# Eight instead of sixteen of a convolution's taps on TensorE, its shifted rows made through device memory, its places one or two slots later

## The chip, the cores and the metric

The kernel runs on one core of a Trainium2 chip. Its time is the device time of one execution in microseconds (us). TensorE (PE) multiplies matrices into PSUM, VectorE (DVE) and ScalarE (ACT) work element by element, GpSimdE (POOL) fills borders and issues some transfers, SyncE (SP) issues most transfers. Every engine works off its own list of instructions, and semaphores hold an instruction back until what it needs is done.

## The reference, cut to what matters

A backbone of two layers works on 640 tokens (128 of a prompt, 512 of a sample) of 1024 channels. Each layer is a feed-forward block, a mixer and a feed-forward block. The mixer of the second, odd layer is this; its depthwise convolution over 31 neighbouring tokens is what the change is about:

```python
def gmlp_conv_mixer(h, w_in, v_ln_g, v_ln_b, sp_w, sp_b, dw_w, dw_b, cn_g, cn_b, w_out):
    u, v, ga, gg = jnp.split(h @ w_in, [D_C, 2 * D_C, 2 * D_C + D_D], axis=-1)
    u = jax.nn.gelu(u)
    v = layer_norm(jax.nn.gelu(v), v_ln_g, v_ln_b)
    vc = v.reshape(b, L // MLP_CHUNK, MLP_CHUNK, N_HEADS_C, HEAD_DIM_C)
    sv = jnp.einsum('hts,bcshd->bcthd', sp_w, vc) + sp_b.T[None, None, :, :, None]
    y_c = u * sv.reshape(b, L, D_C)
    glu = ga * jax.nn.sigmoid(gg)
    y_d = jax.nn.silu(layer_norm(depthwise_conv_centred(glu, dw_w, dw_b), cn_g, cn_b))
    return jnp.concatenate([y_c, y_d], axis=-1) @ w_out
```

## The kernel before, in words

Channels lie on the 128 partitions, tokens along the free axis, so 1024 channels are eight blocks `j`. Tokens are worked in two halves of 320, A and B. All large products are made of three products of rounded halves: a weight tile `wr` is loaded by SP, ScalarE rounds it to `wh` (L217), VectorE takes the rest `wl = wr - wh` (L218), and TensorE multiplies `wh` and `wl` with both halves of the activations (`mm3`, L383 to L385). A unit is one weight tile; two units ahead of the current one are loaded and split.

In `odd`, TensorE's list runs thus. For each block `j` it makes `ga` and `gg` of half A, then of half B; `glu_post` gates them into `pads[j]`, 685 columns with zero borders. Then comes the value product in two rounds of four steps (L1340 to L1342, five PSUM banks at once), then eight `u` units, each followed from the third on by one gate product `sv` (L1360), then the output product, ahead of whose first unit the layer norm's sums over all eight convolution outputs stand (L1396).

Between these stand numbered slots; `bg(slot)` puts convolution `j` at the slot that `CONV_AT` gives: slots 0 to 5 stand behind half A of blocks 2 to 7, slots 6 to 13 behind the eight steps of the value product, slots 14 to 21 among the `u` units. `conv(j)` has three parts. TensorE makes the first `PE_TAPS` taps: four taps at a time, as four row groups of 32 partitions of a tile `R` hold the same 32 channels shifted by 0 to 3 columns, multiplied with a small diagonal matrix `dg` of the tap weights (L1276; 32 instructions a convolution). ScalarE adds the bias and writes `ac` (L1279). VectorE adds the other taps, one scalar_tensor_tensor of 655 columns each (L1283), the last of them in two pieces into `co[j]` (L1288). `rep_next` (L1254) prepares the next convolution's `R` by 16 small copies from SBUF to SBUF (L1261) and its `dg` by one product on VectorE (L1264). One convolution is prepared ahead (`REPS`).

What sets the order: TensorE's list is that of the code. The lists of the other engines are set at build time by a scheduler that goes by priorities; the taps on VectorE have a lowered one (`CONV_LATE`), so the scheduler puts other work first where it reckons it to be ready. At run time each list is worked off as it stands. Tiles called `slab`, `pad`, `cacc`, `diag` share one pool of `OB` buffers (tag `"s"`); PSUM has eight banks.

Of the kernel before, what the change touches and what calls it, by code (L numbers as in the profile page):

```python
# [10 lines left out]
F32 = mybir.dt.float32  # L11
# [5 lines left out]
P = 128  # L17
# [14 lines left out]
NSTD = 3  # L32
TAP_EARLY = 400
NORM_EARLY = 200
PE_TAPS = 16
RW = 655 + PE_TAPS - 4
REPS = 1
OB = 21
XW_EARLY = 600
CONV_LATE = 3000  # L40
CONV_AT = (1, 2, 3, 4, 5, 7, 9, 11)
SV_LAG = 2
LN_STEPS = ((0, 'sum', 0), (0, 'sum', 1), (0, 'mean', 0), (0, 'mean', 1), (3, 'sq', 0), (5, 'sq', 1), (7, 'var', 1), (11, 'var', 0))
Y_AT = (1, 3)
# [28 lines left out]
def build(tc, ap):  # L73
    nc = tc.nc
    V, S, TE, G = nc.vector, nc.scalar, nc.tensor, nc.gpsimd
    ctx = ExitStack()
    with ctx:
# [4 lines left out]
        spool = ctx.enter_context(tc.tile_pool(name="slabs", bufs=8))  # L82
        tpool = ctx.enter_context(tc.tile_pool(name="temps", bufs=10))
        pspool = ctx.enter_context(tc.tile_pool(name="psum", bufs=8, space=PSUM))
        state = {"pool": None, "ctx": None}

        uid = [0]

        def nm(p):
            uid[0] += 1  # L90
            return f"{p}_{uid[0]}"

        def slab(dt=F32, cols=T):
            return state["pool"].tile([P, cols], dt, tag="s", name=nm("slab"))
# [32 lines left out]
        def open_phase(bufs):  # L127
            state["ctx"] = ExitStack()
            state["pool"] = state["ctx"].enter_context(tc.tile_pool(name=nm("phase"), bufs=bufs, reuse_waits="tile"))
# [11 lines left out]
        def psum(cols=512):  # L141
            return pspool.tile([P, cols], F32, tag="ps", name=nm("ps"))
# [13 lines left out]
        def cvc(name, i):  # L156
            o = CV[name] + i
            return cv[:, o:o + 1]
# [310 lines left out]
        def boundary(first_keys, L, isc, ish, prev, kind):  # L469
            need_mod(L, isc)  # L470
            need_mod(L, ish)
            hn = []

            def nxt(H, rs, cs):
                if cs[0] == 0 and H == A:
                    prefetch(index[first_keys[-1]])
                    hn.append(kind())
                for c in cs:
                    if H == A and c < 2:
                        with tc.high_priority(offset=NORM_EARLY):  # L480
                            apply_mod(H, c, rs, L, isc, ish, hn[0])
                    else:
                        apply_mod(H, c, rs, L, isc, ish, hn[0])
            prev(nxt)

            def mid():
                nxt(B, finish(B), range(KC))
            pa = run_units(A, first_keys, hn[0], kouter=True, mid={1: mid})
            close_phase()
            return hn[0], pa  # L490
# [736 lines left out]
        def odd(prev):  # L1227
            first = [("oga", 0), ("ogg", 0), ("oga", 1), ("ogg", 1)]
            hn, pa = boundary(first, 1, 4, 3, prev, Rows)
            open_phase(OB)  # L1230
            ph = state["pool"]
# [12 lines left out]
            pads = {}  # L1244
# [9 lines left out]
            def rep_next():  # L1254
                if not ready or len(reps) == REPS:
                    return
                j = ready.pop(0)
                R = [ph.tile([P, RW], F32, tag="s", name=nm("rep")) for _ in range(4)]
                for r in range(4):
                    for q in range(4):  # L1260
                        nc.sync.dma_start(out=R[q][32 * r:32 * r + 32, :], in_=pads[j][32 * q:32 * q + 32, r:r + RW])  # L1261
                ng = PE_TAPS // 4
                dg = ph.tile([P, ng * 4, 32], F32, tag="s", name=nm("diag"))
                V.tensor_mul(dg, id4[:, None, :].to_broadcast([P, ng * 4, 32]),  # L1264
                             cw[:, j, 0:ng].rearrange("p m q -> p (m q)")[:, :, None].to_broadcast([P, ng * 4, 32]))
                reps[j] = (R, dg)

            def conv(j):
                pad = pads.pop(j)
                R, dg = reps.pop(j)  # L1270
                ac = ph.tile([P, 655], F32, tag="s", name=nm("cacc"))
                for q0, q1 in ((0, 328), (328, 655)):
                    ps = psum()
                    for m in range(PE_TAPS // 4):
                        for q in range(4):
                            TE.matmul(ps[32 * q:32 * q + 32, :q1 - q0], lhsT=dg[:, 4 * m + q, :],  # L1276
                                      rhs=R[q][:, 4 * m + q0:4 * m + q1],
                                      start=(m == 0), stop=(m == PE_TAPS // 4 - 1))
                    S.activation(out=ac[:, q0:q1], in_=ps[:, :q1 - q0], func=AF.Identity, bias=cvc("dw_b", j))  # L1279
                rep_next()  # L1280
                with tc.high_priority(offset=-CONV_LATE):
                    for i in range(PE_TAPS, CONV_D - 1):
                        V.scalar_tensor_tensor(out=ac, in0=pad[:, i:i + 655], scalar=cvc("dw_w", i * 8 + j), in1=ac,  # L1283
                                               op0=ALU.mult, op1=ALU.add)
                    co[j] = slab(F32)
                    i = CONV_D - 1
                    for a, b, d in ((0, 128, 0), (128, 640, 15)):
                        V.scalar_tensor_tensor(out=co[j][:, a:b], in0=pad[:, a + d + i:b + d + i],  # L1288
                                               scalar=cvc("dw_w", i * 8 + j), in1=ac[:, a + d:b + d],
                                               op0=ALU.mult, op1=ALU.add)  # L1290

            def bg(slot):
                for j, at in enumerate(CONV_AT):
                    if at == slot:
                        conv(j)

            def glu_post(H, j, pga, pgg):
                if H == A:
                    t = ph.tile([P, 685], F32, tag="s", name=nm("pad"))
                    for a, b in ((0, 15), (143, 158), (670, 685)):  # L1300
                        G.memset(t[:, a:b], 0.0)
                    pads[j] = t
                sg = tmp()
                S.activation(out=sg, in_=pgg[:, :TH], func=AF.Sigmoid)
                o = SL[H].start
                for (a, b, cond) in SEGS[H]:
                    d = a + 15 if cond == 1 else a + 30
                    V.tensor_mul(pads[j][:, d:d + b - a], sg[:, a - o:b - o], pga[:, a - o:b - o])
                if H == B:
                    ready.append(j)  # L1310
                    rep_next()
# [257 lines left out]
```

## Time and profile before

| | |
|---|---|
| median of 3 runs | 2646.93 us (2642.45 to 2650.54) |
| profiled execution | 2652.95 us, its span 2651.2 us |
| mean granted clock of TensorE | 0.988 |
| ScalarE, GpSimdE busy | 47%, 6% of the span |
| transfers | 378.09 MB, mean 143 GB/s |

The span runs from the first to the last instruction of the profiled execution. A busy time is the time in which an engine had an instruction at work; a wait is the idle time just before an instruction, put down to the one that released it last. The granted clock is the share of TensorE's full clock that the chip allowed.

### The profile page before, as it was taken

The numbers are of one execution on the slowest core, as the hardware profiler recorded it, in microseconds if no ns is written. First come the engines' busy times: TensorE is split into PE (matmuls) and PEld (weight loads), VectorE is DVE, ScalarE is ACT, GpSimd is POOL, SyncE is SP. The second block draws the span as 40 slices with busy tenths as digits, with TensorE's granted clock in tenths as the row PEclk, the third lists the DMA queues.
The fourth block names the chain that finished last, engine by engine and source line by source line (L and its number), as shares of the span: only waits on it lengthen the run. The fifth ranks groups of instructions, "written<-read, shape, count | busy, mean of one in ns | idle before, by whom it ended". The sixth has DMA issues, their size and how long they took to land. (4 is left out here: it accounts for less than half of the span.)

```text
span 2651.2 us, 43728 instructions
## 1 busy us (share of the span) xinstructions
PE 2526.2 (95%) x17229; PEld 2435.4 (92%) x17229; DVE 1936.4 (73%) x3265; ACT 1236.3 (47%) x2310; POOL 154.3 (6%) x255
## 2 busy tenths in 40 slices
PE   7899999899999999999999999999999999999997
PEld 5899999889989999999989999989879998999997
DVE  6878878689996967777597777856885749554465
ACT  4434535458863544445354444533223535444452
POOL 0010110000000010101001011000000000101100
PEclk9999999999999999999999999999999999999999
DMA  7477886222112376877248687724442124656651
GB/s 286 126 215 194 221 222 168 79 70 64 47 54 88 108 200 180 214 195 187 82 125 208 185 227 202 190 80 135 135 110 64 56 72 125 162 144 146 155 123 58
DMA packets 140078, 378.09 MB, mean 143 GB/s; under 512 B 17504, under 2 KB 24160, under 8 KB 139360
## 3 DMA queue, kind: packets, MB, share of 16 engines
q1 hardware_dynamic: 111568, 296.33, 35.4%
q0 software_dynamic: 24768, 71.31, 15.2%
q10 hardware_dynamic: 3536, 7.66, 0.9%
q8 instruction: 135, 2.21, 0.3%
q14 instruction: 71, 0.58, 0.1%
HBM read 329.17 MB, written 3.67 MB: 126 GB/s over the span
## 5 line engine op out<-in xcount | busy, mean ns | idle before, releaser
L218 DVE TENSOR_TENSOR wl<-wr,wh 128x1024 fp32r<-128x1024 f32 (+3 forms) x393 | 390.8, 997 | 301.9 <-ACT wh L217 110.7
L217 ACT CAST wh<-wr 128x1024 fp32r<-128x1024 f32 (+3 forms) x393 | 340.1, 868 | 369.1 <-DMA wr<-in_wd 113.8
L385 PE MATMUL ps<-h,wl 128*128 128x320 f32 x1408 | 438.5, 311 | 9.8 <-DVE wl L218 9.8
L383 PE MATMUL ps<-h,wh 128*128 128x320 f32 x1408 | 438.6, 312 | 8.0 <-ACT h L367 7.9
L384 PE MATMUL ps<-h,wh 128*128 128x320 f32 x1408 | 437.8, 311 | 2.9 <-DVE h L368 2.9
L752 PE MATMUL ps<-th,wh 128*128 128x320 f32 x1216 | 384.0, 316 | 36.4 <-ACT tmp L734 24.5
L752 PE MATMUL ps<-quad,wh 128*128 128x320 f32 x1824 | 406.3, 311 | 1.6 <-ACT tmp L734 1.5
L752 PE MATMUL ps<-th,wl 128*128 128x320 f32 x1216 | 381.9, 314 | 3.7 <-DVE wl L218 3.7
L752 PE MATMUL ps<-tl,wh 128*128 128x320 f32 x1216 | 381.1, 313 | 0.0
L314 DVE CUSTOM_DVE_ANT_0 junk<-wm,crow,cv 128x1024 bf16<-128x1024 f32 x256 | 327.7, 1280 | 3.3 <-DMA wm<-in_wm 0.7
L383 PE MATMUL ps<-pair,wh 128*128 128x320 f32 (+1 forms) x976 | 307.6, 315 | 4.6 <-ACT pair L376 1.5
L752 PEld LDWEIGHTS ps<-quad,wh 128*128 128x128 f32 x1824 | 307.5, 189 | 2.3 <-ACT tmp L734 2.3
L384 PE MATMUL ps<-pair,wh 128*128 128x320 f32 (+1 forms) x976 | 302.7, 310 | 1.6 <-DVE pair L378 1.4
L385 PE MATMUL ps<-pair,wl 128*128 128x320 f32 (+1 forms) x976 | 302.4, 310 | 0.0
L752 PE MATMUL ps<-quad,wl 128*128 128x320 f32 x912 | 283.2, 311 | 4.7 <-DVE wl L218 4.7
L385 PEld LDWEIGHTS ps<-h,wl 128*128 128x128 f32 x1408 | 265.9, 189 | 14.0 <-DVE wl L218 14.0
L383 PEld LDWEIGHTS ps<-h,wh 128*128 128x128 f32 x1408 | 266.1, 189 | 10.2 <-ACT h L367 9.9
L752 PEld LDWEIGHTS ps<-th,wh 128*128 128x128 f32 x1216 | 232.9, 191 | 44.0 <-ACT tmp L734 30.8
L384 PEld LDWEIGHTS ps<-h,wh 128*128 128x128 f32 x1408 | 266.0, 189 | 5.0 <-DVE h L368 4.6
L218 DVE TENSOR_TENSOR wl<-ws,wh 128x1024 fp32r<-128x1024 f32 x152 | 185.6, 1221 | 90.7 <-ACT wh L217 38.5
L752 PEld LDWEIGHTS ps<-th,wl 128*128 128x128 f32 x1216 | 233.0, 192 | 5.5 <-DVE wl L218 5.5
L752 PEld LDWEIGHTS ps<-tl,wh 128*128 128x128 f32 x1216 | 232.9, 192 | 0.0
(261 smaller groups left out, 4380.4 us busy)
## 6 DMA issues: line engine op xcount, KB each, us to landing
wm<-in_wm SPq DMA_DIRECT2D x128, 512.0 KB, 4.4
wr<-in_wgu SPq DMA_DIRECT2D x76, 512.0 KB, 4.9
ws<-in_wgu SPq DMA_DIRECT2D x152, 256.0 KB, 4.2
ws<-in_wgu POOLq DMA_DIRECT2D x76, 512.0 KB, 6.0
x<-y POOLq DMA_DIRECT2D x96, 320.0 KB, 6.1
wr<-in_wd SPq DMA_DIRECT2D x64, 384.0 KB, 3.5
wr<-in_wd SPq DMA_DIRECT2D x64, 320.0 KB, 3.9
wr<-in_wgu SPq DMA_DIRECT2D x76, 256.0 KB, 3.7
```

What stands on the lines that cost most here:

```text
L217: S.copy(hi, src)
L218: state["paced"] = V.tensor_sub(lo, src, hi).ins
L314: V.tensor_tensor_reduce(out=junk[0], in0=w, in1=crow[cond], scale=1.0, scalar=cvc("b_mod", L * 72 + idx * KC + c), op0=ALU.mult, op1=ALU.add,
L383: TE.matmul(ps, lhsT=wh, rhs=xh, start=start, stop=False)
L384: TE.matmul(ps, lhsT=wh, rhs=xl, start=False, stop=False)
L385: TE.matmul(ps, lhsT=wl, rhs=xh, start=False, stop=stop)
L752: TE.matmul(ps[:, :TH], lhsT=l[k], rhs=r[:, k, :], start=(first and k == 0 and n == 0), stop=(k == 3 and n == 2), skip_group_check=True)
```

## The change

`PE_TAPS` goes from 16 to 8: TensorE's part of a convolution is 16 instructions instead of 32, and VectorE adds taps 8 to 30 instead of 16 to 30, that is 22 full-length instructions and the last tap in two pieces instead of 14 and the last. `R` is one tile with a buffer of its own; `rep_next` writes `pads[j]` to a `row` in device memory and reads it back by four transfers, one for each shift, that fill all four column groups. The pool of slabs has 17 instead of 21 buffers. The convolutions stand at slots 2, 3, 4, 5, 7, 9, 11, 13: the first to fourth one slot later, the last four two slots later.

```diff
--- before.py
+++ after.py
@@ -32,13 +32,13 @@
 NSTD = 3
 TAP_EARLY = 400
 NORM_EARLY = 200
-PE_TAPS = 16
+PE_TAPS = 8
 RW = 655 + PE_TAPS - 4
 REPS = 1
-OB = 21
+OB = 17
 XW_EARLY = 600
 CONV_LATE = 3000
-CONV_AT = (1, 2, 3, 4, 5, 7, 9, 11)
+CONV_AT = (2, 3, 4, 5, 7, 9, 11, 13)
 SV_LAG = 2
 LN_STEPS = ((0, 'sum', 0), (0, 'sum', 1), (0, 'mean', 0), (0, 'mean', 1), (3, 'sq', 0), (5, 'sq', 1), (7, 'var', 1), (11, 'var', 0))
 Y_AT = (1, 3)
@@ -82,6 +82,7 @@
         spool = ctx.enter_context(tc.tile_pool(name="slabs", bufs=8))
         tpool = ctx.enter_context(tc.tile_pool(name="temps", bufs=10))
         pspool = ctx.enter_context(tc.tile_pool(name="psum", bufs=8, space=PSUM))
+        dpool = ctx.enter_context(tc.tile_pool(name="rows", bufs=1, space=bass.MemoryType.DRAM))
         state = {"pool": None, "ctx": None}
 
         uid = [0]
@@ -1255,10 +1256,12 @@
                 if not ready or len(reps) == REPS:
                     return
                 j = ready.pop(0)
-                R = [ph.tile([P, RW], F32, tag="s", name=nm("rep")) for _ in range(4)]
+                R = ph.tile([P, 4, RW], F32, tag="rep", name=nm("rep"), bufs=REPS)
+                row = dpool.tile([P, 685], F32, tag="pad", name=nm("row"), bufs=2)
+                nc.sync.dma_start(out=row, in_=pads[j])
                 for r in range(4):
-                    for q in range(4):
-                        nc.sync.dma_start(out=R[q][32 * r:32 * r + 32, :], in_=pads[j][32 * q:32 * q + 32, r:r + RW])
+                    nc.sync.dma_start(out=R[32 * r:32 * r + 32, :, :],
+                                      in_=row[:, r:r + RW].rearrange("(q p) w -> p q w", p=32))
                 ng = PE_TAPS // 4
                 dg = ph.tile([P, ng * 4, 32], F32, tag="s", name=nm("diag"))
                 V.tensor_mul(dg, id4[:, None, :].to_broadcast([P, ng * 4, 32]),
@@ -1274,7 +1277,7 @@
                     for m in range(PE_TAPS // 4):
                         for q in range(4):
                             TE.matmul(ps[32 * q:32 * q + 32, :q1 - q0], lhsT=dg[:, 4 * m + q, :],
-                                      rhs=R[q][:, 4 * m + q0:4 * m + q1],
+                                      rhs=R[:, q, 4 * m + q0:4 * m + q1],
                                       start=(m == 0), stop=(m == PE_TAPS // 4 - 1))
                     S.activation(out=ac[:, q0:q1], in_=ps[:, :q1 - q0], func=AF.Identity, bias=cvc("dw_b", j))
                 rep_next()
```

The change also moves VectorE's list. In the rows below, `cacc` are taps, the last `slab` rows of a `cacc` its last tap, `wl` weight splits, `pad` gatings; the numbers are those of buffers. VectorE, before, at the second convolution (of `pad_18839`):

```order
L1283 SCALAR_TENSOR_TENSOR cacc_19367<-pad_18839,cv,cacc_19367 128x655 x2
L1264 TENSOR_TENSOR diag_19424<-id_18829,cw 128x512
L1283 SCALAR_TENSOR_TENSOR cacc_19367<-pad_18839,cv,cacc_19367 128x655
L218 TENSOR_TENSOR wl_19499<-wr_19496,wh_19498 128x1024
L1283 SCALAR_TENSOR_TENSOR cacc_19367<-pad_18839,cv,cacc_19367 128x655 x3
L218 TENSOR_TENSOR wl_19506<-wr_19503,wh_19505 128x1024
L1308 TENSOR_TENSOR pad_19359<-tmp_19493,ps_19443 128x320
L1283 SCALAR_TENSOR_TENSOR cacc_19367<-pad_18839,cv,cacc_19367 128x655 x8
L1288 SCALAR_TENSOR_TENSOR slab_19440<-pad_18839,cv,cacc_19367 128x128
```

After, from the second convolution's first taps (of `pad_18841`) on to the `diag` of the fourth:

```order
L1286 SCALAR_TENSOR_TENSOR cacc_19458<-pad_18841,cv,cacc_19458 128x655 x2
L219 TENSOR_TENSOR wl_19569<-wr_19566,wh_19568 128x1024
L1286 SCALAR_TENSOR_TENSOR cacc_19458<-pad_18841,cv,cacc_19458 128x655 x3
L1311 TENSOR_TENSOR pad_19450<-tmp_19563,ps_19513 128x320
L219 TENSOR_TENSOR wl_19576<-wr_19573,wh_19575 128x1024
L1286 SCALAR_TENSOR_TENSOR cacc_19458<-pad_18841,cv,cacc_19458 128x655 x17
L1291 SCALAR_TENSOR_TENSOR slab_19510<-pad_18841,cv,cacc_19458 128x128
L1311 TENSOR_TENSOR pad_19628<-tmp_19632,ps_19572 128x128
L1311 TENSOR_TENSOR pad_19628<-tmp_19632,ps_19572 128x192
L1267 TENSOR_TENSOR diag_19664<-id_18831,cw 128x256
```

Before, the `diag` for the third convolution stood two taps into the second and 14 taps ran in pieces of 2, 1, 3 and 8. Now 22 taps run in pieces of 2, 3 and 17, and the next `diag`, that of the fourth convolution, stands behind all of them.

VectorE, before, from the seventh convolution (`cacc_20330`), with the `diag` of the eighth in the second row:

```order
L1283 SCALAR_TENSOR_TENSOR cacc_20330<-pad_19757,cv,cacc_20330 128x655 x2
L1264 TENSOR_TENSOR diag_20387<-id_18829,cw 128x512
L1283 SCALAR_TENSOR_TENSOR cacc_20330<-pad_19757,cv,cacc_20330 128x655 x5
L218 TENSOR_TENSOR wl_20550<-wr_20547,wh_20549 128x1024
L1283 SCALAR_TENSOR_TENSOR cacc_20330<-pad_19757,cv,cacc_20330 128x655 x6
L218 TENSOR_TENSOR wl_20586<-wr_20583,wh_20585 128x1024
L1283 SCALAR_TENSOR_TENSOR cacc_20330<-pad_19757,cv,cacc_20330 128x655
L1288 SCALAR_TENSOR_TENSOR slab_20403<-pad_19757,cv,cacc_20330 128x128
L1288 SCALAR_TENSOR_TENSOR slab_20403<-pad_19757,cv,cacc_20330 128x512
```

After, from the sixth convolution (`cacc_20138`) to the `diag` of the eighth:

```order
L219 TENSOR_TENSOR wl_20374<-wr_20371,wh_20373 128x1024
L1286 SCALAR_TENSOR_TENSOR cacc_20138<-pad_19450,cv,cacc_20138 128x655 x16
L219 TENSOR_TENSOR wl_20478<-wr_20475,wh_20477 128x1024
L1286 SCALAR_TENSOR_TENSOR cacc_20138<-pad_19450,cv,cacc_20138 128x655 x4
L1349 BN_STATS vst<-vbig 128x6
L1286 SCALAR_TENSOR_TENSOR cacc_20138<-pad_19450,cv,cacc_20138 128x655
L1349 BN_STATS vst<-vbig 128x6 x4
L1351 BN_AGGR vmv<-vst 128x2 x5
L219 TENSOR_TENSOR wl_20537<-wr_20534,wh_20536 128x1024
L1291 SCALAR_TENSOR_TENSOR slab_20190<-pad_19450,cv,cacc_20138 128x128
L1291 SCALAR_TENSOR_TENSOR slab_20190<-pad_19450,cv,cacc_20138 128x512
L1267 TENSOR_TENSOR diag_20308<-id_18831,cw 128x256
```

The `diag` of the eighth convolution stood two taps into the seventh; now it stands ahead of the seventh's taps but behind all of the sixth's, with splits and norm steps among them.

VectorE, before, from the last taps of the eighth convolution to the first gate product:

```order
L1283 SCALAR_TENSOR_TENSOR cacc_20493<-pad_19956,cv,cacc_20493 128x655 x2
L1350 RECIPROCAL vrs<-vrs 128x5
L1288 SCALAR_TENSOR_TENSOR slab_20544<-pad_19956,cv,cacc_20493 128x128
L1352 TENSOR_SCALAR vbig<-vbig,vmv,vrs 128x1024 x5
L218 TENSOR_TENSOR wl_20762<-wr_20759,wh_20761 128x1024
L1288 SCALAR_TENSOR_TENSOR slab_20544<-pad_19956,cv,cacc_20493 128x512
L218 TENSOR_TENSOR wl_20834<-wr_20831,wh_20833 128x1024
L218 TENSOR_TENSOR wl_20906<-wr_20903,wh_20905 128x1024
L1365 SCALAR_TENSOR_TENSOR slab_20825<-ps_20818,cv,spb 128x384
L1365 SCALAR_TENSOR_TENSOR tmp_20828<-ps_20819,cv,spb 128x256
L1367 TENSOR_TENSOR slab_20672<-slab_20672,slab_20825 128x384
```

After, from the first tap of the eighth convolution to the first gate product (L1368 and L1370) and the next split:

```order
L1286 SCALAR_TENSOR_TENSOR cacc_20407<-pad_19806,cv,cacc_20407 128x655
L1368 SCALAR_TENSOR_TENSOR tmp_20662<-ps_20653,cv,spb 128x256
L1286 SCALAR_TENSOR_TENSOR cacc_20407<-pad_19806,cv,cacc_20407 128x655 x21
L1291 SCALAR_TENSOR_TENSOR slab_20450<-pad_19806,cv,cacc_20407 128x128
L1291 SCALAR_TENSOR_TENSOR slab_20450<-pad_19806,cv,cacc_20407 128x512
L1370 TENSOR_TENSOR slab_20506<-slab_20506,tmp_20662 128x256
L1368 SCALAR_TENSOR_TENSOR slab_20659<-ps_20652,cv,spb 128x384
L1370 TENSOR_TENSOR slab_20506<-slab_20506,slab_20659 128x384
L219 TENSOR_TENSOR wl_20812<-wr_20809,wh_20811 128x1024
```

Before, the eighth convolution ended ahead of the first gate product, with three splits between. Now all but one of its 22 taps stand between the two halves of that product's first step, and the split follows.

## Rows read from the trace of the kernel before

**Rows 1.** Page, busy us (share of the span) and instructions of each engine.

```profile
PE 2526.2 (95%) x17229; PEld 2435.4 (92%) x17229; DVE 1936.4 (73%) x3265; ACT 1236.3 (47%) x2310; POOL 154.3 (6%) x255
```

**Rows 2.** Table by stretch: from:to, us, busy of each engine, PEclk, DMA share, GB/s.

```profile
1841.56:1998.88 157.32, 157.32 (x1190) 124.81 (x1189) 139.12 (x179) 38.52 (x55) 0.58 (x9) 1.00 0.45 121
1998.88:2064.30 65.42, 65.42 (x469) 65.30 (x471) 32.63 (x57) 21.22 (x35) 0.00 (x0) 1.00 0.20 65
```

**Rows 3.** Waits of TensorE, 1780 to 2200: us in total, times, longest.

```profile
PE ps L385 <- DVE wl L218: 3.5, 4, 0.9
```

**Rows 4.** Chain that ended last, odd mixer: start us, us, what.

```profile
1841.56 4.54 PE ps L1276 x64
1860.38 4.54 PE ps L1276 x64
...
2036.47 1.11 PE ps L1360 x10
...
2064.30 2.29 PE ps L1396 x32
```

**Rows 5.** Timeline of VectorE: start us, us, engine line op out<-in xcount.

```profile
1846.82 0.90 DVE L1283 SCALAR_TENSOR_TENSOR cacc<-pad,cv,cacc 128x655 f32<-128x655 f32 x1 [2.54 <-ACT cacc L1279]
1847.64 0.68 DVE L1264 TENSOR_TENSOR diag<-id,cw 128x512 f32<-128x512 f32 x1
1848.24 1.83 DVE L1283 SCALAR_TENSOR_TENSOR cacc<-pad,cv,cacc 128x655 f32<-128x655 f32 x2
1849.99 1.22 DVE L218 TENSOR_TENSOR wl<-wr,wh 128x1024 fp32r<-128x1024 f32 x1
1851.13 2.77 DVE L1283 SCALAR_TENSOR_TENSOR cacc<-pad,cv,cacc 128x655 f32<-128x655 f32 x3
...
1855.39 7.45 DVE L1283 SCALAR_TENSOR_TENSOR cacc<-pad,cv,cacc 128x655 f32<-128x655 f32 x8
1862.87 0.35 DVE L1288 SCALAR_TENSOR_TENSOR slab<-pad,cv,cacc 128x128 f32<-128x128 f32 x1
1863.14 0.55 DVE L1308 TENSOR_TENSOR pad<-tmp,ps 128x128 f32<-128x128 f32 x2
1863.60 0.74 DVE L1288 SCALAR_TENSOR_TENSOR slab<-pad,cv,cacc 128x512 f32<-128x512 f32 x1
...
1930.68 2.15 DVE L1329 SCALAR_TENSOR_TENSOR spb<-ps,cv,spb 128x128 f32<-128x128 f32 x8
...
1961.89 3.06 DVE L1346 BATCH_NORM_STATS2 vst<-vbig 128x6 f32<-128x512 f32 x5
...
2004.52 3.70 DVE L1352 TENSOR_SCALAR vbig<-vbig,vmv,vrs 128x1024 f32<-128x1024 f32 x5
```

**Rows 6.** Timeline of TensorE, second feed-forward block of the odd layer, around a wait.

```profile
2244.96 0.31 PE L752 MATMUL ps<-tl,wh 128*128 128x320 f32 x1
2245.11 0.31 PE L752 MATMUL ps<-th,wl 128*128 128x320 f32 x1
2248.81 0.42 PE L752 MATMUL ps<-th,wh 128*128 128x320 f32 x1 [3.40 <-ACT wh L217]
...
2252.19 0.47 PE L752 MATMUL ps<-th,wl 128*128 128x320 f32 x1
2252.46 0.47 PE L752 MATMUL ps<-th,wh 128*128 128x320 f32 x1
```

**Rows 7.** Table by stretch, behind that wait.

```profile
2250.61:2253.79 3.18, 3.18 (x14) 3.18 (x13) 0.00 (x0) 0.42 (x1) 0.00 (x0) 0.50 0.99 305
```

**Rows 8.** DMA issues: out<-in engine op xcount, KB each, median us to landing.

```profile
x<-y POOLq DMA_DIRECT2D x96, 320.0 KB, 6.1
...
rep<-pad SPq DMA_DIRECT2D x128, 83.4 KB, 2.6
...
out_s<-fin SPq DMA_DIRECT2D x8, 128.0 KB, 2.2
```

**Rows 9.** Timeline of SP's queue, the first convolution's copies.

```profile
1821.95 12.94 SPq L1261 DMA_DIRECT2D rep<-pad  x16
```

## The prediction

> **What bounds the kernel now.** I read the page's busy times first [rows 1]: TensorE is busy 95% of the span, VectorE 73%. That is a mean over stages, so the next view is the table by stretch around the change [rows 2]. In the odd mixer, from the first convolution on TensorE (1841.56) to the first sum of the layer norm over its outputs (2064.30), TensorE is busy for all of 157.32 + 65.42 = 222.74 us at a granted clock of 1.00. VectorE is busy for 139.12 of the first 157.32 us and for 32.63 of the last 65.42 us. The reader is to see two things: TensorE sets the pace here, and VectorE is already 88% full while the eight convolutions run and only half full afterwards. The waits of TensorE confirm it: over the whole mixer its matmuls waited 3.5 us in all for a weight split `wl` [rows 3]. The chain of waits gives TensorE's milestones [rows 4]: one convolution takes 4.54 us, the next place is 18.82 us later (1860.38 - 1841.56), the gate's third product (`sv`) stands at 2036.47, the layer norm's first sum at 2064.30, 27.83 us behind it. The timeline of VectorE prices everything else [rows 5].
>
> **What is taken off TensorE.** A convolution's matmuls fall from 32 to 16, so 4.54 us become 2.27; over eight convolutions 18.2 us leave an engine that is busy without a gap. If nothing else were late, that would be the gain.
>
> **What is put on VectorE.** Taps 8 to 15 of every convolution become scalar_tensor_tensor instructions: 8 x 8 = 64 more. Eight in a row took from 1855.39 to 1862.87 [rows 5], so 0.935 us each, since each waits for the one before it; 64 of them are 59.8 us. The diagonal `diag` shrinks from 512 to 256 columns. That form is not in the trace; it costs between nothing and the 0.60 us from 1847.64 to 1848.24 [rows 5]; I take half of that with some fixed cost, 0.33.
>
> **What the order makes of it.** VectorE takes its instructions in the order shown above, so what TensorE needs from it (a `diag`, a weight split, a product that frees a PSUM bank) comes when the taps ahead of it are done. The sum is therefore VectorE's work from the first tap of the first convolution up to the gate's first product, which frees the PSUM bank that TensorE's third product waits for.
>
> The start: the first convolution moves from slot 1 to slot 2, and slot 1 is empty. Slot 2 lies at 1860.38 - 4.54 = 1855.84; 2.27 us later the matmuls are through, at 1858.11. From the end of the matmuls to the first tap it was 0.72 us before (1841.56 + 4.54 = 1846.10, tap at 1846.82 [rows 4, 5]). First tap: 1858.83, 12 us later than before, with 64 more taps to do.
>
> The work in that stretch of the new order, durations from start to start in [rows 5]:
> 176 taps (22 per convolution) x 0.935 = 164.6; a tap followed by an instruction that doesn't need it gives way after 0.82 instead (1849.99 - 1848.24 = 1.75 for two), which some 21 splits and other pieces do: -2.5. The eight last taps in two pieces, 0.27 (1862.87 to 1863.14) and 0.74 less 0.08 of overlap: 7.4. 19 weight splits at 1.14 (1849.99 to 1851.13): 21.7. Pad products of seven half units, 0.46 for the pair of half A (1863.14 to 1863.60), somewhat less for the one of half B: 3.0. Six diagonals: 2.0. Eight products for `spb`: 2.1. Ten batch_norm_stats (five in 3.06): 6.0. Five aggregates and a reciprocal: 0.5. The five `vbig` rows (3.70): 3.6. The gate's three instructions up to that product (of 256 and 384 columns, between the pieces of 128 and 512 columns with 0.35 and 0.74): 1.3. Together 209.7 us, and the place is reached at 1858.83 + 209.7 = 2068.5.
>
> For TensorE alone the same place would come at 2036.47 - 18.2 = 2018.3. VectorE is 50 us later, and TensorE stands for those 50 us, in pieces. Per slot VectorE needs 22 x 0.935 + 0.93 + 2 x 1.14 + 0.86 + 0.33 = 25.0 us, TensorE 14.28 + 2.27 = 16.55, so it falls 8.4 us back each time. The splits are ordered two units ahead and stay in time for a while; the first to be late is the fourth convolution, at 1855.84 + 3 x 16.55 = 1905.5, whose `diag` stands behind all taps of the second, at some 1907. The long waits follow in the value product: its fourth PSUM bank is held until pad and `spb` products behind nineteen taps of the third convolution are done, and the seventh and eighth convolutions wait for a `diag` that stands behind all taps of the fifth and the sixth, 10 to 13 us each. The last is that of the third gate product, some 6 us.
>
> From the gate's third product on, TensorE has the same work as before: 27.8 us [rows 4]. The layer norm's first sum comes at 2068.5 + 27.8 = 2096.3 instead of 2064.30: **+32.0 us**. All convolution outputs are ready by then, so nothing of them is late a second time, and behind that place both orders are the same.
>
> **The clock.** After an idle time of 3.40 us before 2248.81, the granted clock was 0.50 (1.2 GHz) from 2250.61 to 2253.79 and matmuls started every 0.27 us instead of 0.15 [rows 6, 7]: 12 of them, 1.4 us lost; call it 1.5. Four of the new waits (fourth bank, seventh and eighth convolution, third gate product) are longer than that idle time. The first three are followed by another wait for VectorE, which swallows the loss; the last, of some 6 us ahead of the third product, is not: +1.5. The Trainium skill, in "TensorE: Matmul & The Clock Gate" (HAM oscillation), says the same of every such gap: each idle gap that is long enough makes the engine start again at half clock. If each of the four were on the path, the term would be 6.0 and the sum 4.5 us more.
>
> **Transfers.** The sixteen 83 KB copies per convolution held SP's queue for 12.94 us [rows 9]; five issues of the same kind hold it for some 4. Nothing waited for SP, so that is worth nothing. The new way is a write to device memory, then four reads of 330 KB, which can't start before the write has landed and the previous convolution has left the single `rep` buffer, with weight loads queued behind them on SP. The trace shows writes landing in 2.2 us, and transfers of 320 KB, the slowest of that size, in 6.1 [rows 8]. One behind the other that is 2.2 + 4 x 6.1 = 26.6 us, all at once 2.2 + 6.1 = 8.3; the old copies, sixteen at once, landed in 2.6 [rows 8], so I take the end near 8.3, under the 16.55 us of a slot and far under VectorE's 25.0. Cost nothing, hidden behind the wait for VectorE. "DMA: Bandwidth & Descriptors" of the Trainium skill (Anatomy of one DMA) warns that a write to device memory can be slow to report itself complete; by its fixed cost of about 2 us the write would change nothing here. The slabs go from 21 to 17 because four copies leave them: no change. ScalarE issues the same instructions.
>
> **Sum.** 2652.95 (the profiled execution: span 2651.2 and 1.75 around it) + 32.0 + 1.5 = 2686.5. That execution is 6.0 us over the median of the runs, 2646.93, so the forecast on the median is 2646.93 + 33.5 = 2680.4, rounded to 2681.
>
> **Rivals.**
> - *TensorE's saving counts* (faster): VectorE keeps up and 18.2 us go: 2629. For it: TensorE is the engine without gaps, and VectorE is idle half of the time behind the convolutions [rows 2]. Against it: between first tap and third product TensorE would leave VectorE 2018.3 - 1858.8 = 159.5 us for 209.7 us of work. It decides only if a tap costs less than 0.935 - 50.2/176 = 0.65 us; the trace shows 0.94. Chance 0.04.
> - *Only the end counts*: the third gate product finds a free bank (eight banks, two for each product, two for the unit beside it), the later units run on, and VectorE's backlog only has to be gone when the layer norm starts. Its whole work up to there is 209.7 + four splits 4.6 + the rest of the gate 12.6 + eight output splits 5.9 = 232.8, done at 2091.6; before, the layer norm started 5 us ahead of the last output splits, so +22: 2669. With some pieces of the order kinder than I read them it gives +5 to +24. Chance 0.07, of which 0.02 ends within 0.3%.
> - *The transfers or the clock add to it*: with the four reads one behind the other, 26.6 us exceed a slot's 25.0, and with the shorter distance in the value product convolutions wait for `rep` on top of `diag`; with all four clock losses +4.5. 2686 to 2700. Chance 0.12.
> - The forecast, +27 to +41: 0.77.
>
> **Chances and range.** Differences of under 0.3% (8 us) can't be told from none here. Faster 0.04, same 0.02, slower 0.94. The range: the bounds of the diagonal (-2.0 to +1.6), of the clock (0 to 6.0) and of the overlap terms give +29 to +39; it is widened below to the case where only the end counts and above to that of late transfers: 2669 to 2697.
>
> **What would show it.** Right: VectorE without idle time from the first tap to the last convolution's end; TensorE idle for about 50 us in the mixer, released by VectorE (`diag`, a PSUM bank, little by `wl`), none of it by `rep`; 22 taps per convolution at 0.93 us; from the gate's third product to the layer norm's first sum 28 us as before. Wrong: the seventh and eighth convolutions on time; convolution matmuls released by `rep`; a layer norm that starts before 2085 or after 2110; any difference ahead of slot 1 or behind the mixer.

## The result and the profile after

The changed kernel took 2679.99 us (median of 4 runs, 2669.69 to 2681.81), the kernel before, in the same comparison, 2644.69 us: ratio 1.013, 95% interval 1.0111 to 1.0149. Forecast were 2681 us and +33.5 us; the medians differ by 35.3.

The page's first line, busy times of the changed kernel, against [rows 1]:

```profile
PE 2519.7 (94%) x16973; PEld 2433.6 (91%) x16973; DVE 1991.4 (74%) x3329; ACT 1235.1 (46%) x2310; POOL 154.3 (6%) x255
```

256 rows of matmuls fewer: the profile shows each of the 8 x 16 instructions that are gone as two. 64 VectorE instructions and 55.0 us more on VectorE. TensorE, once busy through the whole mixer, now waits. Its waits from 1790 to 2100 (total us, times, longest), where the kernel before waited 1.6 us in all (the 3.5 us of [rows 3] lie behind 2100):

```profile
PE ps L1279 <- issue: 13.0, 2, 10.6
PE ps L1343 <- DVE pad L1311: 10.4, 1, 10.4
PE ps L1279 <- DVE diag L1267: 9.0, 1, 9.0
PE ps L1363 <- DVE slab L1368: 4.5, 1, 4.5
PE ps L384 <- DVE tmp L1368: 1.9, 1, 1.9
PE ps L1363 <- ACT cacc L1282: 1.6, 1, 1.6
```

L1279 are convolution matmuls, L1343 the value product, L1363 the gate products, L384 a `u` unit. The 13.0 us that the view puts down to "issue" are waits for a `diag` too, as VectorE's timeline shows. First the stretch from the first tap on, against [rows 5]:

```profile
1850.80 3.71 DVE L1286 SCALAR_TENSOR_TENSOR cacc<-pad,cv,cacc 128x655 f32<-128x655 f32 x4 [1.59 <-ACT cacc L1282]
...
1882.72 15.95 DVE L1286 SCALAR_TENSOR_TENSOR cacc<-pad,cv,cacc 128x655 f32<-128x655 f32 x17
...
1899.44 0.42 DVE L1267 TENSOR_TENSOR diag<-id,cw 128x256 f32<-128x256 f32 x1
...
1905.78 17.82 DVE L1286 SCALAR_TENSOR_TENSOR cacc<-pad,cv,cacc 128x655 f32<-128x655 f32 x19
...
1924.92 0.55 DVE L1311 TENSOR_TENSOR pad<-tmp,ps 128x128 f32<-128x128 f32 x2
...
1980.75 0.42 DVE L1267 TENSOR_TENSOR diag<-id,cw 128x256 f32<-128x256 f32 x1
...
2009.58 0.42 DVE L1267 TENSOR_TENSOR diag<-id,cw 128x256 f32<-128x256 f32 x1
...
2039.55 0.48 DVE L1368 SCALAR_TENSOR_TENSOR tmp<-ps,cv,spb 128x256 f32<-128x256 f32 x1
2039.94 19.68 DVE L1286 SCALAR_TENSOR_TENSOR cacc<-pad,cv,cacc 128x655 f32<-128x655 f32 x21
...
2060.93 0.61 DVE L1368 SCALAR_TENSOR_TENSOR slab<-ps,cv,spb 128x384 f32<-128x384 f32 x1
```

TensorE's timeline at six of its waits (start, us; in brackets the idle time before and its releaser):

```profile
1899.96 4.10 PE L1279 MATMUL ps<-rep,diag 128*32 128x328 f32 x32 [2.37 <-issue]
...
1925.52 0.79 PE L1343 MATMUL ps<-wh,pair 128*128 128x512 f32 x1 [10.44 <-DVE pad L1311]
...
1981.27 4.50 PE L1279 MATMUL ps<-rep,diag 128*32 128x328 f32 x32 [9.02 <-DVE diag L1267]
...
2010.20 3.70 PE L1279 MATMUL ps<-rep,diag 128*32 128x328 f32 x32 [10.61 <-issue]
...
2040.08 0.59 PE L384 MATMUL ps<-pair,wh 128*128 128x320 f32 x1 [1.92 <-DVE tmp L1368]
...
2061.60 2.50 PE L1363 MATMUL ps<-spw,vbig 128*128 128x128 f32 x10 [4.52 <-DVE slab L1368]
```

Read the two side by side: the diagonals of 1899.44, 1980.75 and 2009.58 end 0.1 to 0.2 us before the fourth, seventh and eighth convolution start; each stands behind a row of taps. The `pad` that holds the fourth bank of the value product stands behind nineteen of them. The last row of VectorE's timeline is the second half of the gate's first product, behind 21 taps; TensorE's third product starts right behind it, at 2061.60. The table by stretch, first tap to that product and on to the layer norm's first sum, against [rows 2]:

```profile
1850.80:2061.54 210.74, 170.36 (x1061) 143.38 (x1059) 204.28 (x259) 44.59 (x66) 0.00 (x0) 0.90 0.37 100
2061.54:2092.39 30.85, 30.79 (x208) 30.67 (x212) 17.75 (x32) 7.63 (x14) 0.00 (x0) 0.90 0.20 69
```

VectorE is busy for 204.28 of 210.74 us; one idle time of 0.46 us aside, nearly all of the rest is the 0.04 us between two taps of which one waits for the other (0.90 us each, started some 0.94 apart).

One offset has to be taken out first. The sum that opens the mixer's norm stands here in the two timelines, before and after:

```profile
1781.17 0.70 PE L359 MATMUL ps<-tmp,ones_d 128*128 128x320 f32 x2
```

```profile
1773.26 0.70 PE L360 MATMUL ps<-tmp,ones_d 128*128 128x320 f32 x2
```

The changed kernel reaches it 7.9 us sooner. No edit lies ahead of it, and over all kernels below it moves between 1772.70 and 1785.12 without any tie to what they change; it is the scatter of single executions. The mixer itself is measured from it to the layer norm's first sum: 2064.2 - 1781.2 = 283.0 us before, 2092.3 - 1773.3 = 319.0 after, +36.0. With -7.9 ahead and +0.7 behind that makes the 28.8 us between the two spans. The 36.0 are made up thus: TensorE waits 40.4 us more (41.4 against 1.0) and works 17.6 us less for want of the matmuls, but 13.1 us longer at a lowered clock; these two are read from kernel a below, which has the same matmuls, 1.0 us of waits and a granted clock of 1.00 (busy 282.0 us before, 277.5 here, 264.4 in a).

### The profile page after: what moved, and what is told of

Its sections match the earlier page's. It is cut to its first block, busy times and chain, and to the rows that moved or that the text cites. A ratio compares the mean times of both kernels' runs of the same rounds, so it can differ in the third digit from the quotient of the medians.

```text
span 2680.0 us, 43167 instructions
## 1 busy us (share of the span) xinstructions
PE 2519.7 (94%) x16973; PEld 2433.6 (91%) x16973; DVE 1991.4 (74%) x3329; ACT 1235.1 (46%) x2310; POOL 154.3 (6%) x255
## 5 line engine op out<-in xcount | busy, mean ns | idle before, releaser
L384 PE MATMUL ps<-h,wh 128*128 128x320 f32 x1408 | 438.8, 312 | 7.5 <-ACT h L368 7.5
L384 PE MATMUL ps<-pair,wh 128*128 128x320 f32 (+1 forms) x976 | 310.7, 318 | 6.0 <-DVE tmp L1368 1.9
L384 PEld LDWEIGHTS ps<-h,wh 128*128 128x128 f32 x1408 | 266.2, 189 | 9.6 <-ACT h L368 9.3
```

Of the source, the lines that this page charges most:

```text
L384: TE.matmul(ps, lhsT=wh, rhs=xh, start=start, stop=False)
```

## The experiments

Theory 1: the time follows VectorE's work, from the first tap to the gate product that frees a bank for TensorE. Rivals: the transfers and the single `rep` buffer; the later slots; the waits for diagonals as prices of their own; VectorE's whole work up to the layer norm. "In the mixer" is the stretch just defined, of one profiled execution, less that of before; the executions of g and i were among the shortest of their kernels, that of k among the longest.

| kernel | ratio of times, 95% interval | in the mixer, us |
|---|---|---|
| the change | 1.013 (1.0111 to 1.0149) | +36.0 |
| a, 64 taps left out | 0.993 (0.9906 to 0.9954) | -17.6 |
| b, slots of before | 1.0095 (1.0065 to 1.0124) | +26.6 |
| c, diagonals ahead | 1.0119 (1.0096 to 1.0142) | +31.1 |
| d, 16 taps, new rows | 1.000 (0.9983 to 1.0018) | 0.0 |
| e, 16 taps, later slots | 1.0003 (0.9988 to 1.0018) | 0.0 |
| f, 12 taps, later slots | 1.0096 (1.0079 to 1.0114) | +20.4 |
| g, 12 taps, slots of before | 1.0019 (1.0007 to 1.0031) | +1.1 |
| h, 16 to 8 taps | 0.9984 (0.9972 to 0.9996) | -6.5 |
| i, as f, eighth one late | 1.0009 (0.9994 to 1.0024) | +0.2 |
| j, 8 taps, two late | 1.0058 (1.0035 to 1.0081) | +12.2 |
| k, 16 to 8 taps, two late | 0.9976 (0.9962 to 0.999) | -7.2 |

Each ratio is to runs of the kernel before in the same comparison. For a to d these had a median of 2651.9 us, 7.2 above the 2644.69 that the ranges in us were set by. So the medians of a (2633.88) and c (2682.86) lie just above the ranges expected, and that of b (2676.76) in the range of its rival; by the ratio, put on 2644.69, they are 2626, 2676 and 2670 us, inside the ranges of theory 1 (b's interval, 2662 to 2677, just touches its rival).

**a: the added taps left out.**

```diff
-                    for i in range(PE_TAPS, CONV_D - 1):
+                    for i in range(PE_TAPS + 8, CONV_D - 1):
```

> The changed kernel, but VectorE adds only taps 16 to 30: taps 8 to 15 of every convolution are left out (64 instructions fewer), all else stays. Theory 1 (VectorE's work between the first tap and the gate's first product sets the time): 59.8 us leave 210.7 us of work, VectorE would be there at 2001.7 of the changed kernel's time axis, TensorE alone, with its 18.2 us off, only at 2010.4; TensorE bounds, its waits in the mixer fall from 43 us to under 6, and the time is 18 us under the kernel before: 2627 (2622 to 2633). Theory 2 (the new transfers, the single buffer of shifted rows or the later slots make TensorE wait): those are all still there, so waits of the convolutions stay at 10 us or more and the time stays at 2645 to 2670.

2633.88 against 2651.9 us, 18.0 less, and 17.6 less in the mixer: what the matmuls left TensorE. From 1790 to 2100 TensorE waits 1.0 us in all. Rows, buffer and slots were those of the change, so none of them costs anything while VectorE has the time.

**d and e: the new rows alone, the later slots alone**, each on the kernel before (d also with its pool of 17).

```diff
-PE_TAPS = 8
+PE_TAPS = 16
-CONV_AT = (2, 3, 4, 5, 7, 9, 11, 13)
+CONV_AT = (1, 2, 3, 4, 5, 7, 9, 11)
```

(d, against the changed kernel)

> The kernel before with the shifted rows made through device memory alone (one write, four reads, one buffer, 17 slabs); 16 taps on TensorE and the slots of before. Theory 1: the transfers are hidden: as before, 2645 (2639 to 2650), and no convolution matmul waits for its rows. Rival (the reads, 6.3 us from issue to landing instead of 2.6, and one buffer make convolutions late where the slots stand 14 us apart): 2 to 5 us for several of the eight, 2655 to 2670.

```diff
-CONV_AT = (1, 2, 3, 4, 5, 7, 9, 11)
+CONV_AT = (2, 3, 4, 5, 7, 9, 11, 13)
```

(e, against the kernel before)

> The kernel before with the convolutions at the later slots (2, 3, 4, 5, 7, 9, 11, 13) alone. Theory 1: with 16 taps VectorE has 59.8 us less to do; from a first tap 14.3 us later its work ends some 20 us ahead of the gate's third product, so TensorE still bounds: as before (within 0.3%, ratio 0.997 to 1.003), TensorE's waits in the mixer under 6 us. Rival (the later slots by themselves cost, since the last convolutions now stand right ahead of the gate): 5 to 14 us more.

Both take the time of before, and the mixer's length is the same to a tenth. In d the DMA issues (KB each, median us to landing) read:

```profile
rep<-row SPq DMA_DIRECT2D x32, 333.5 KB, 6.1
row<-pad SPq DMA_DIRECT2D x8, 342.5 KB, 4.5
```

10.6 us one behind the other, against 2.6 for the old copies [rows 8], and yet hidden where the convolutions stand 18.4 to 18.8 us apart.

**b: eight taps at the slots of before.**

```diff
-CONV_AT = (2, 3, 4, 5, 7, 9, 11, 13)
+CONV_AT = (1, 2, 3, 4, 5, 7, 9, 11)
```

> The changed kernel with the convolutions at the slots of before (1, 2, 3, 4, 5, 7, 9, 11). Theory 1: VectorE starts its taps one slot, 14.3 us, earlier with the same work, so the gate's first product and the end come up to 14 us earlier: 2666 (2663 to 2672). Rival (what counts is that each diagonal stands behind the taps of the convolution two before it, and the single buffer; both are unchanged, and the convolutions wait as much longer as they start earlier): 2680 (2676 to 2684). If earlier places make the waits worse: over 2684.

26.6 instead of 36.0 us in the mixer: 9.4 of the 14.3 us come back. The slots cost nothing in e and 9 us here: their place counts only where VectorE sets the pace. Of the missing 5, 2.7 are work that the scheduler now puts ahead of the product (213.4 instead of 210.7 us from first tap to product). The rest is behind it: TensorE waited last not for the third product but for the first half of the first, 4.2 us.

**c: the diagonals computed ahead.**

```diff
-                dg = ph.tile([P, ng * 4, 32], F32, tag="s", name=nm("diag"))
-                V.tensor_mul(dg, ...)
-                reps[j] = (R, dg)
+                reps[j] = (R, diags[:, j])
...
+            for j in range(8):
+                V.tensor_mul(diags[:, j], ...)
```

> The changed kernel with all eight diagonals computed ahead of the first convolution into a tile of their own (slabs 17 to 16). Theory 1: the waits of the fourth, seventh and eighth convolution (2.4, 9.0 and 10.6 us) for a diagonal go, but VectorE's sum loses only 7 x 0.33 = 2.3 us, so the same time is waited for later, at the gate products: 2677 (2674 to 2681), with a longer wait behind the value product. Rival (the waits for the diagonals are the price themselves): 22 us go, 2658 (2654 to 2664).

The convolutions' 22 us of waits for diagonals are gone, and the time is not. TensorE's waits in c:

```profile
PE ps L384 <- DVE tmp L1369: 19.3, 1, 19.3
PE ps L1344 <- DVE pad L1309: 12.8, 1, 12.8
PE ps L1277 <- DMA rep<-row: 5.7, 2, 3.1
PE ps L1364 <- DVE slab L1369: 2.8, 1, 2.8
```

The same wait moved to the gate, since the product on VectorE came after 208.4 us of work, 2.3 less than 210.7. With the diagonals out of the way the reads of `rep` show, 5.7 us, and are swallowed as well: VectorE was busy through them, for 202.0 of the 208.4 us. The mixer is 4.9 us shorter: 2.3 of work, and 2.7 behind the product, where c lost nothing to the clock:

```profile
2066.20:2094.30 28.10, 28.02 (x205) 27.90 (x205) 17.70 (x32) 8.60 (x15) 0.00 (x0) 1.00 0.23 76
```

**f and g: twelve taps on TensorE**, at the slots of the change and at those of before (b's edit).

```diff
-PE_TAPS = 8
+PE_TAPS = 12
```

> The changed kernel with twelve taps on TensorE instead of eight. Theory 1: 32 taps, 29.9 us, leave VectorE's 210.7 us, the diagonals add 1.2, the first tap comes 1.1 us later; so the gate's third product stands some 6 us behind its time in the kernel before, and the end with it: ratio to before 1.002 to 1.004 (+6 to +10 us with the clock's loss). Rival (the loss is a matter of the slots and the new rows and not of the number of taps): as the changed kernel, +25 or more. Rival (TensorE's saving counts): 9 us less.

> Twelve taps on TensorE at the slots of before, rows through device memory. Theory 1: VectorE reaches the gate's products as early as TensorE does with its 9.1 us off; what is left are single waits in the value product for a bank and for a diagonal: between 6 us less than before and 1 more, most likely 3 less (ratio 0.999). Rival (what is put on VectorE always comes back in full): +10 or more.

f missed by 10 us and more. g, with +1.1 us in the mixer, lies at the upper end of what was expected: 3.8 us for the fourth bank of the value product, 2.8 for `rep` and some 2.7 of clock (busy 276.4 us, against 273.7 in k with as many matmuls) took TensorE's gain. By its time g missed: the whole interval lies above the +1 us that was allowed. Its profiled execution, 2649.97 us, is shorter than its median, 2655.74; why the others are longer is not on record. VectorE's work in f was 2044.4 - 1863.8 = 180.6 us, near the 182.0 reckoned; the place was wrong. (f also waited 5.8 us for `rep`, ahead of the longer wait for VectorE.) TensorE, in its timeline, stood at the `u` unit right behind the first product, two units ahead of the third product:

```profile
2042.91 0.64 PE L384 MATMUL ps<-pair,wh 128*128 128x320 f32 x1 [17.02 <-DVE tmp L1368]
```

and VectorE's timeline says why:

```profile
2022.16 4.71 DVE L1286 SCALAR_TENSOR_TENSOR cacc<-pad,cv,cacc 128x655 f32<-128x655 f32 x5
...
2027.92 6.51 DVE L1286 SCALAR_TENSOR_TENSOR cacc<-pad,cv,cacc 128x655 f32<-128x655 f32 x7
...
2035.48 5.58 DVE L1286 SCALAR_TENSOR_TENSOR cacc<-pad,cv,cacc 128x655 f32<-128x655 f32 x6
...
2042.38 0.48 DVE L1368 SCALAR_TENSOR_TENSOR tmp<-ps,cv,spb 128x256 f32<-128x256 f32 x1
...
2043.77 0.61 DVE L1368 SCALAR_TENSOR_TENSOR slab<-ps,cv,spb 128x384 f32<-128x384 f32 x1
```

The product has two halves in two banks. In the changed kernel the half of 256 columns stood 21 taps ahead of the other (2039.55 and 2060.93), its bank served that unit, and only the third product waited for the second half. In f both stand behind the eighth convolution, and TensorE waits with 45.7 us still to come (2042.9 to 2088.6) instead of 30.9. So the work has to be summed to the first bank that TensorE lacks.

**i: as f, but the eighth convolution behind the first gate product.**

```diff
-CONV_AT = (2, 3, 4, 5, 7, 9, 11, 13)
+CONV_AT = (2, 3, 4, 5, 7, 9, 11, 17)
```

> The kernel with twelve taps and the later slots, with the eighth convolution moved from slot 13 to slot 17, behind the gate's first product (the matmuls, the taps and the splits stay the same in number). It took 1.0096 of the kernel before, and TensorE waited 17.0 us in one piece for the first half of that product, which stood on VectorE behind the eighth convolution's taps. Theory 1, as mended (what counts is the VectorE work that stands ahead of the first gate product to free a bank, not all of it): about 17.8 us of taps go behind the product, the wait of 17.0 us is gone and all but some 5 us of the excess with it: ratio 1.001 to 1.004. Rival (VectorE's whole work up to the layer norm counts, which is unchanged): 1.008 to 1.011.

Not a tap fewer, and 20 of the 20.4 us are gone; the ratio lies a hair under the range. VectorE in i:

```profile
2013.13 0.61 DVE L1368 SCALAR_TENSOR_TENSOR slab<-ps,cv,spb 128x384 f32<-128x384 f32 x1
2013.66 0.47 DVE L1368 SCALAR_TENSOR_TENSOR tmp<-ps,cv,spb 128x256 f32<-128x256 f32 x1
...
2019.47 0.90 DVE L1286 SCALAR_TENSOR_TENSOR cacc<-pad,cv,cacc 128x655 f32<-128x655 f32 x1 [2.98 <-ACT cacc L1282]
```

TensorE's wait for a gate product fell from 17.0 to 0.8 us, though one convolution now waited 4.7 us for earlier taps; the eighth convolution's taps run to 2040 beside the `u` units, ahead of the layer norm at 2056. The rival that counts all of VectorE's work falls.

**j: eight taps, the seventh and eighth convolution late.**

```diff
-CONV_AT = (2, 3, 4, 5, 7, 9, 11, 13)
+CONV_AT = (1, 2, 3, 4, 5, 7, 11, 17)
```

> Eight taps at the slots of before, but the seventh convolution at 11 and the eighth at 17 (1, 2, 3, 4, 5, 7, 11, 17). With 1, 2, 3, 4, 5, 7, 9, 11 it took 1.0095. Theory 1, as mended: one convolution's 22 us of taps go behind the first gate product; the waits of the value product and the fourth and fifth convolution (some 21 us) stay, TensorE's 18.2 us stand against them: +8 to +14 us, ratio 1.003 to 1.0055. Rival (VectorE's whole work counts): 1.008 to 1.011.

As expected: the 12.2 us that stay are waits (8.3 in the value product, 7.6 and 2.4 for earlier diagonals, 3.6 at the gate, 21.9 in all) and 7.9 of clock, less the 17.6 that left TensorE. The ratio itself lies just above the expected range, its interval over most of it.

**h and k: fewer taps moved, and those late.** In both the number of taps is a list, h at b's slots, k at j's.

```diff
-PE_TAPS = 8
+PE_TAPS = 16
+TAPS = (16, 16, 12, 16, 12, 12, 12, 8)
...
-                    for m in range(PE_TAPS // 4):
+                    for m in range(TAPS[j] // 4):
...
-                    for i in range(PE_TAPS, CONV_D - 1):
+                    for i in range(TAPS[j], CONV_D - 1):
```

(k: 16, 12, 16, 12, 12, 12, 8, 8; the diagonals go by the same list, `PE_TAPS` is left as the width of the rows)

> The slots of before, rows through device memory, and 16, 16, 12, 16, 12, 12, 12, 8 taps on TensorE: 24 taps move to VectorE (22.4 us), late in the stretch, 6.8 us leave TensorE. Theory 1: VectorE's work ends some 9 us ahead of the gate's third product, so TensorE's saving counts in full: 5 to 10 us less than before, ratio 0.996 to 0.998, and TensorE waits for VectorE under 6 us in the mixer. Rival (any tap moved to VectorE is late somewhere): no less than before.

> 16, 12, 16, 12, 12, 12, 8, 8 taps on TensorE, rows through device memory, slots 1, 2, 3, 4, 5, 7, 11, 17: 32 taps move to VectorE, 9.1 us leave TensorE, and the gate's first product stands ahead of the eighth convolution's taps. Theory 1, as mended: TensorE waits under 6 us in the mixer and its saving counts in full: 7 to 11 us less than before, ratio 0.996 to 0.9975. Rival (taps put on VectorE are late somewhere): 0.998 or more.

h waits 1.6 us from 1790 to 2100, no more than before, and its mixer is 6.5 us shorter, as much as TensorE's busy time fell. k waits 2.6 us and gains 7.2. In the whole time k is faster than before, 2644.02 against 2649.01 us, by 0.1 to 0.4%, and h by 0.04 to 0.3%; both ratios stand a hair above their ranges. k has the lowest ratio of the complete kernels here, but its interval and h's overlap, so that k beats h isn't shown.

## Why the prediction was right

Step by step, the trace put on the axis of before by adding 7.9 us:

| step | forecast | measured |
|---|---|---|
| first tap | 1858.83 | 1858.71 |
| fourth convolution late, until | 1907 | 1907.9 |
| VectorE's work to the gate's product | 209.7 | 210.7 |
| that product | 2068.5 | 2069.4 |
| from it to the layer norm's first sum, clock included | 27.8 + 1.5 | 30.9 |
| layer norm's first sum | 2097.8 | 2100.3 |

The mechanism held: a shows that without the added taps there is no loss, d and e that rows and slots by themselves carry none, c that the diagonals' waits are only where VectorE's lateness shows. On top of the taps the later slots do count, with 9.4 of the 36.0 us (b), since VectorE starts later; the forecast had that in its first tap, 12 us late. The predicted waits are there, 2.4, 10.4, 9.0 and 10.6 us, the last 4.5 instead of some 6, and nothing waits for `rep`. VectorE's list was counted right: 176 taps, 19 splits, six diagonals, and the form of `diag` that no row showed cost 0.33 us, as taken (1899.44 to 1899.77, where VectorE goes on). Against the mixer's 36.0 us the forecast's 33.5 is short by two small errors of one sign: 1.0 us of VectorE's work and 1.5 of the clock. That the medians' 35.3 came within 2 us is in part luck: four executions of the changed kernel alone lie 12 us apart.

The clock is the term on the path that was mis-sized. After the last wait of 4.52 us TensorE ran at a granted clock of 0.50 (1.2 GHz) in a first piece and at 1.00 again later:

```profile
2061.60:2065.00 3.40, 3.40 (x15) 3.40 (x16) 3.40 (x7) 0.00 (x0) 0.00 (x0) 0.50 0.15 45
2065.00:2072.72 7.72, 7.72 (x47) 7.72 (x47) 2.91 (x6) 0.44 (x1) 0.00 (x0) 0.84 0.32 116
2072.72:2092.39 19.67, 19.67 (x150) 19.55 (x153) 11.41 (x20) 7.20 (x13) 0.00 (x0) 1.00 0.16 55
```

The third product and the unit behind it took 2072.72 - 2061.60 = 11.1 us, the next such pair, at full clock, 8.16 (to 2080.88): 3.0 lost, where the one stretch of before had been read as 1.5. That the losses at the earlier waits are swallowed was right: the fourth, seventh and eighth convolution took 4.10, 4.50 and 3.70 instead of 2.41 us, and the gate's product on VectorE came when VectorE's sum said. These halved stretches are part of the 50 us that TensorE was to stand: idle, it shows 40.4 us more than before, and of the 13.1 us of clock 10.1 lie ahead of the third product, 50.5 together.

Two terms off the path were mis-sized as well. The write of a `row` took 6.0 us to land, not 2.2, and the way through device memory 12.3, not 8.3; hidden all the same. And eight convolutions left TensorE 17.6 us, not 18.2.

Two sentences of the forecast were too simple. "Any difference ahead of slot 1" was named as a sign against it; 7.9 us were there, and they are scatter. And the place of the last wait was right by the order of this build only: had the first half of the product stood behind the eighth convolution's taps, as in f, TensorE would have waited with 45.7 us to go after the end of those taps, by an estimate from these two kernels some 14 us worse. The case "only the end counts" was given 0.07 with TensorE finding free banks; i shows that it takes an order that puts the gate ahead of the taps.

## What to carry to other kernels

Work moved from a full engine to a half-idle one is priced in the stretch where it lands, by summing the second engine's list up to the first instruction that the first engine waits for; a share of busy time over the whole mixer would have promised a gain (VectorE's 210.2 us before and 59.8 more fit into its 283.0). Waits along the way were symptoms here: taking the diagonals' away only moved it to the next place. What paid was to move as much as fits (h, k), and to place it behind the instructions that free banks, even at the cost of starting later (i, j, k); the gain of 0.1 to 0.4% is small beside the loss of 1.3%.

## What the runs showed of the hardware

A convolution of sixteen matmuls takes 2.41 us, not half of the 4.61 that thirty-two take in the same view; twenty-four take 3.51. The write of a `row` took 6.0 us to land in the changed kernel and 4.5 in d, two to three times the 2.2 of the smaller writes in [rows 8], and the four reads behind it 6.3 and 6.1, so the way through device memory takes 10 to 12 us. The length of a wait alone didn't decide TensorE's clock: after 2.37 us of idle time a convolution ran at 0.59, after 2.80 us in c the stretch behind stood at 1.00. What decided it was not tried.
